# Experts of a mixture ranked by token count on the chip, six light ones in plain float32 on two column tiles

## The chip, the cores and the metric

The kernel runs on one core of one Trainium2 chip. The metric is the device time of one execution in microseconds, as the median of several runs. TensorE (PE) multiplies, VectorE (DVE), ScalarE (ACT) and GpSimd (POOL) work on elements, SyncE (SP) issues most of the transfers, and 16 DMA engines move the data.

## What is computed

A trunk of two residual layers over 512 tokens of 1024 channels. Layer 0 mixes tokens by a state-space scan and a pooling mixer, layer 1 by stick-breaking attention. After each mixer comes a mixture of 16 experts, and that is where the change lies:

```
for i in range(DEPTH):                                  # DEPTH = 2
    ...
    x = layer_norm(DEEPNORM_ALPHA * x + mix, ln_mix_g[i], ln_mix_b[i])
    ple = (p[i] @ ple_w_proj[i]) * sigmoid(x @ ple_w_gate[i])
    ffn = grouped_moe(x, router_w, router_bias, moe_w1[i], moe_w3[i], moe_w2[i])
    x = layer_norm(DEEPNORM_ALPHA * x + ffn + ple, ln_ffn_g[i], ln_ffn_b[i])

def grouped_moe(...):                                   # gates: best group of 4, its best 2 experts
    h = silu(einsum('td,edf->etf', xt, w1)) * einsum('td,edf->etf', xt, w3)
    h = h * gates.T[:, :, None]
    y = einsum('etf,efd->td', h, w2)
```

An expert has w1 and w3 of 1024 x 512 and w2 of 512 x 1024, all float32. Each token goes to two experts, so 1024 pairs of token and expert are spread over 16 experts in each layer.

## The kernel before

The reference is in float32. The kernel makes each product of three matmuls in the faster format fp32r: every operand is split into a rounded high part and a low part that holds the rest (`split`, line 81: ScalarE copies the high part, VectorE subtracts), and `mm3` (line 85) adds high x high, high x low and low x high in PSUM.

`route` (line 797 on) works out for every token its two experts, counts the tokens of each expert by a matmul with ones, and `lists` (line 897) turns this into a list of rows for each expert. An expert has CAP = 96 places; entries past its last token point out of bounds, and transfers skip them. If any expert has more than 96 tokens, a flag is set and `overflow` (line 1131, a branch of all engines after expert 12) works off the rest; otherwise the branch only costs its test.

`ffn` (line 915) writes x to a buffer `xd` in DRAM, GpSimd gathers an expert's rows from there into `xgs` (`gather`), `load_g` transposes them on PE and splits them into `g`. For each expert, `up` multiplies with w1 and w3 (two halves of the 1024 channels, kh, into two PSUM banks), `act` makes silu(h1) x h3, `turn` transposes the result, `down` multiplies with w2 (two halves of the output), and `scatter` writes the rows to `yd`. The loop at line 1043 overlaps two experts: while expert e goes through act, turn and down, the first half of up of expert e+1 is multiplied, and the second half after that. The experts come in the order 0 to 15. After expert 7 stands a block of the ple gate (`gate`, GATES); after the loop the rows of `yd` are loaded and added.

Weights come in units of 1 MB (128 x 2048 float32), six for an expert: w1 and w3 for each kh, and two halves of w2. `plan_ffn` (line 1223) lists the units in the order of use, `prefetch` (line 95) issues their loads on SP in that order, LA = 6 units ahead of use (3 from expert 13 on), and `weights` (line 109) splits a unit in two halves into ring buffers. Units lie in the pool `raw` of 17 slots, which X (4 slots), xt (2), xg, pT and g (2) share. A load waits in SP's queue until its slot has been read out, which for a unit of weights is the end of its split. Every address is known when the program is built, so loads may run ahead of the routing.

`plain` (line 474) is like `weights`, without a split: the unit is read from its slot as float32.

## Time and profile before

| | us |
|---|---|
| median of three runs | 1232.31 (1230.9 to 1234.02) |
| the profiled execution | 1232.32 |
| its span | 1230.7 |
| PE busy | 1162.8 (94%) |
| VectorE busy | 959.1 (78%) |
| ScalarE busy | 750.9 (61%) |
| GpSimd busy | 134.9 (11%) |

The profile gives busy time by engine, and, in 40 slices of the span, the busy share of each engine and of the DMA engines in tenths, with the bytes that these moved. A busy PE here includes the drain of each matmul, which overlaps the next one, so matmuls are timed from the start of one to the start of the next. "Waits" put the idle time before an instruction down to the one that released it. PEclk is the clock granted to TensorE, 1.00 for 2.4 GHz and 0.50 for 1.2 GHz.

### The profile page before, as it was taken

The numbers are of one execution on the slowest core, as the hardware profiler recorded it, in microseconds if no ns is written. First come the engines' busy times: TensorE is split into PE (matmuls) and PEld (weight loads), VectorE is DVE, ScalarE is ACT, GpSimd is POOL, SyncE is SP. The second block draws the span as 40 slices with busy tenths as digits, with TensorE's granted clock in tenths as the row PEclk, the third lists the DMA queues.
The fourth block names the chain that finished last, engine by engine and source line by source line (L and its number), as shares of the span: only waits on it lengthen the run. The fifth ranks groups of instructions, "written<-read, shape, count | busy, mean of one in ns | idle before, by whom it ended". The sixth has DMA issues, their size and how long they took to land. (4 is left out here: it accounts for less than half of the span.)

```text
span 1230.7 us, 17431 instructions
## 1 busy us (share of the span) xinstructions
PE 1162.8 (94%) x6479; PEld 888.6 (72%) x6479; DVE 959.1 (78%) x1381; ACT 750.9 (61%) x1063; POOL 134.9 (11%) x150
## 2 busy tenths in 40 slices
PE   6967999999999999999999999999999999999995
PEld 4856779777768776777777767688877767777674
DVE  6997866798986998785576467755799896989786
ACT  4322542688876888763465456523488885888761
POOL 5010020111010101100000000011101100011101
PEclk9998999999999999999999999998999999999998
DMA  8225662599996998972121024434299998899971
GB/s 254 69 78 184 223 232 97 183 372 377 379 377 247 357 388 325 355 283 69 35 76 63 1 69 153 150 145 163 61 361 387 385 378 304 287 397 356 305 276 70
DMA packets 158166, 285.13 MB, mean 232 GB/s; under 512 B 19584, under 2 KB 43664, under 8 KB 157008
## 3 DMA queue, kind: packets, MB, share of 16 engines
q1 hardware_dynamic: 143760, 256.56, 58.5%
q0 software_dynamic: 9568, 25.19, 6.0%
q10 hardware_dynamic: 4736, 2.10, 0.6%
q8 instruction: 55, 0.90, 0.3%
q14 instruction: 47, 0.39, 0.1%
HBM read 272.02 MB, written 20.19 MB: 237 GB/s over the span
## 5 line engine op out<-in xcount | busy, mean ns | idle before, releaser
L83 DVE TENSOR_TENSOR w_0l<-raw,w_0h 128x1024 fp32r<-128x1024 f32 (+1 forms) x233 | 280.0, 1202 | 53.7 <-ACT w_0h L82 49.4
L82 ACT ACTIVATE w_0h<-raw 128x1024 fp32r<-128x1024 f32 (+1 forms) x233 | 242.5, 1041 | 41.2 <-PE pA L89 22.2
L83 DVE TENSOR_TENSOR w_2l<-raw,w_2h 128x1024 fp32r<-128x1024 f32 x205 | 249.8, 1218 | 15.9 <-ACT w_2h L82 15.5
L82 ACT ACTIVATE w_2h<-raw 128x1024 fp32r<-128x1024 f32 x205 | 216.6, 1057 | 49.7 <-PE pA L89 40.3
L87 PE MATMUL pA<-w_0h,g 128*96 128x512 f32 x256 | 104.2, 407 | 0.8 <-ACT g L82 0.7
L88 PE MATMUL pA<-w_0l,g 128*96 128x512 f32 x256 | 101.2, 395 | 1.8 <-DVE w_0l L83 1.8
L89 PE MATMUL pA<-w_0h,g 128*96 128x512 f32 x256 | 101.5, 397 | 0.3 <-DVE g L83 0.3
L89 PE MATMUL pA<-w_2h,g 128*96 128x512 f32 x256 | 101.5, 397 | 0.0
L87 PE MATMUL pA<-w_2h,g 128*96 128x512 f32 x256 | 101.1, 395 | 0.0
L88 PE MATMUL pA<-w_2l,g 128*96 128x512 f32 x256 | 100.3, 392 | 0.0
L979 POOL DMA_INDIRECT yd<-ysb,ixm x30 | 37.7, 1256 | 441.9 <-ACT ysb L1052 421.4
L89 PEld LDWEIGHTS pA<-w_0h,g 128*96 128x96 f32 x256 | 41.3, 161 | 18.8 <-DVE g L83 2.1
L88 PEld LDWEIGHTS pA<-w_2l,g 128*96 128x96 f32 x256 | 41.5, 162 | 17.9
L89 PEld LDWEIGHTS pA<-w_2h,g 128*96 128x96 f32 x256 | 41.3, 161 | 18.0
L87 PEld LDWEIGHTS pA<-w_2h,g 128*96 128x96 f32 x256 | 41.3, 161 | 17.7
L88 PEld LDWEIGHTS pA<-w_0l,g 128*96 128x96 f32 x256 | 41.6, 163 | 17.2 <-DVE w_0l L83 3.8
L973 POOL DMA_INDIRECT xg<-xd,ixm x32 | 37.4, 1170 | 149.0 <-PE pT L995 79.1
L87 PEld LDWEIGHTS pA<-w_0h,g 128*96 128x96 f32 x256 | 41.5, 162 | 15.7 <-ACT g L82 3.1
L87 PE MATMUL pB<-w_0h,sT 128*96 128x512 f32 x128 | 50.7, 396 | 1.2 <-ACT sT L82 1.2
L679 DVE TENSOR_TENSOR_SCAN kw<-kw 128x128 f32<-128x128 f32 (+3 forms) x64 | 50.2, 813 | 0.9 <-ACT kw L676 0.6
L88 PE MATMUL pB<-w_0l,sT 128*96 128x512 f32 x128 | 50.5, 394 | 0.4 <-DVE w_0l L83 0.4
L89 PE MATMUL pB<-w_0h,sT 128*96 128x512 f32 x128 | 50.8, 397 | 0.0
(442 smaller groups left out, 2810.9 us busy)
## 6 DMA issues: line engine op xcount, KB each, us to landing
raw<-in_moe_w_dram SPq DMA_DIRECT2D x192, 1024.0 KB, 10.1
raw<-in_sb_w_qkv_dram SPq DMA_DIRECT2D x12, 1024.0 KB, 5.1
raw<-in_ple_w_gate_dram SPq DMA_DIRECT2D x8, 1024.0 KB, 8.4
yt<-yd SPq DMA_DIRECT2D x8, 1024.0 KB, 8.1
raw<-in_ab_w_out_dram SPq DMA_DIRECT2D x4, 1024.0 KB, 6.4
xd<-x0r POOLq DMA_DIRECT2D x8, 512.0 KB, 4.1
raw<-in_sb_w_out_dram SPq DMA_DIRECT2D x4, 1024.0 KB, 5.6
raw<-in_ab_w_in_dram SPq DMA_DIRECT2D x3, 1024.0 KB, 7.7
```

The lines of the kernel that those rows point to most:

```text
L82: return (self.nc.scalar.activation(hi, src, AF.Copy), (self.nc.gpsimd if pool else self.nc.vector).tensor_tensor(lo, src, hi.bitcast(F32) ...
L83: (self.nc.gpsimd if pool else self.nc.vector).tensor_tensor(lo, src, hi.bitcast(F32), op=OP.subtract))
L87: t.matmul(out, s[0], m[0], start=first, stop=False)
L88: t.matmul(out, s[0], m[1], start=False, stop=False)
L89: t.matmul(out, s[1], m[0], start=False, stop=last)
L679: v.tensor_tensor_scan(rv, rv, rv, 1.0, op0=OP.mult, op1=OP.min)
L973: return nc.gpsimd.indirect_dma_start(out=xgs[:CAP, e % 2, :], out_offset=None, in_=xd[:, :], in_offset=bass.IndirectOffsetOnAxis(ap=self. ...
L979: nc.gpsimd.indirect_dma_start(out=yd[:, :], out_offset=bass.IndirectOffsetOnAxis(ap=self.iy[:CAP, e:e + 1], axis=0), in_=src[:CAP], in_of ...
```

## The change

After the counts are known, `route` ranks the experts by them on VectorE: `key` is 16 x count plus a tie-break, raised for experts 0 and 1 so that they take ranks 1 and 2 always; `rank` is the number of keys that are at least as large. The lists are made by rank instead of by expert (`val`), and `order` holds, as integers, the expert of each rank. The loop goes through ranks in the order of SEQ, so that position 0 and 1 are experts 0 and 1, and ranks 11 to 16, the light ones, stand at positions 2, 5, 8, 10, 12 and 14. A light expert has 64 places instead of 96; the flag of the overflow counts 32 more for it.

Since which expert has rank 3 to 16 is known only on the chip, `expert` reads its index from `order` into a register of SP, and `prefetch` issues the loads of its weights at an address made from it. Loads of experts 0 and 1 stay as they were.

A light expert is not split: its gathered rows are copied out of PSUM as float32 (one half by ScalarE, the other by VectorE), the weights are read by `plain`, and `up` multiplies each 128 channels of g with w1 and with w3 in turn, one to PSUM partitions 0 to 63, the other to 64 to 127 of the same bank: two tiles of 64 columns of the array. `down` does the same with the two halves of w2. A slot of weights is now free when PE has read it. `last_onehot` and `overflow` use the ranks too. Cut to what matters:

```diff
+SMALL = 64
+BIG = 10
+SEQ = (1, 2, 11, 3, 4, 12, 5, 6, 13, 7, 14, 8, 15, 9, 16, 10)
...
+            if callable(ap):
+                ap = ap()
+                if ap is None:
+                    break
...
+        self.kb = cp.tile([128, 16], F32, name="kb")
+        nc.vector.tensor_copy(self.kb, self.w16)
+        for e in range(2):
+            nc.vector.tensor_scalar(self.kb[:, e:e + 1], self.kb[:, e:e + 1], float((2 - e) << 15), None, op0=OP.add)
...
-        v.tensor_reduce(red[:, 0], pp[:, 64:80], AX.X, OP.max)
-        self.flag = cp.tile([128, 1], I32, tag="flag", bufs=2, name=f"flag{layer}")
-        v.tensor_scalar(self.flag, red[:, 0], CAP + 0.5, None, op0=OP.is_gt)
-        keep = cp.tile([128, 2, NT, 17], F32, tag="keep", bufs=1, name=f"keep{layer}")
-        pos = keep[:, :, :, 16:17]
...
+        key, rank, cap = f(16), f(16), f(16)
+        cmp = rt[:, 0:256].rearrange("p (a b) -> p a b", a=16)
+        val = rt[:, 256:384].rearrange("p (k i e) -> p k i e", k=2, i=NT)
+        sq16 = [128, 16, 16]
+        v.scalar_tensor_tensor(key, pp[:, 64:80], 16.0, self.kb, op0=OP.mult, op1=OP.add)
+        v.tensor_tensor(cmp, key[:, None, :].to_broadcast(sq16), key[:, :, None].to_broadcast(sq16), op=OP.is_ge)
+        v.tensor_reduce(rank, cmp, AX.X, OP.add)
+        fk = lambda ap: ap.rearrange("p k i e -> p (k i) e")
+        bc8 = [128, 2 * NT, 16]
+        v.tensor_tensor(fk(val), fk(m), rank[:, None, :].to_broadcast(bc8), op=OP.mult)
+        v.tensor_reduce(fk(rk), fk(val), AX.X, OP.add)
+        v.tensor_tensor(fk(val), self.slotrow[:, None, :16].to_broadcast(bc8), fk(rk).to_broadcast(bc8), op=OP.is_equal)
+        for k in range(2):
+            v.tensor_tensor(val[:, k], val[:, k], self.tokv[:, :, k:k + 1].to_broadcast(bc16), op=OP.mult)
...
-        self.val = val = keep[:, :, :, :16]
-        for k in range(2):
-            v.tensor_tensor(val[:, k], m[:, k], self.tokv[:, :, k:k + 1].to_broadcast(bc16), op=OP.mult)
...
-        self.lists(0, tiles)
+        self.lists(pos, val, tiles)
+        v.tensor_tensor(cmp, self.slotrow[:, :16][:, :, None].to_broadcast(sq16), rank[:, None, :].to_broadcast(sq16),
+                        op=OP.is_equal)
+        v.tensor_tensor(cmp, cmp, self.w16[:, None, :].to_broadcast(sq16), op=OP.mult)
+        v.tensor_reduce(key, cmp, AX.X, OP.add)
+        order = cp.tile([128, 16], I32, tag="order", bufs=1, name=f"order{layer}")
+        v.tensor_scalar(order, key, -1.0, 16.0, op0=OP.mult, op1=OP.add)
+        self.order[layer] = order
+        v.tensor_scalar(cap, rank, BIG + 0.5, float(CAP - SMALL), op0=OP.is_gt, op1=OP.mult)
+        v.tensor_tensor(cap, cap, pp[:, 64:80], op=OP.add)
+        v.tensor_reduce(red[:, 0], cap, AX.X, OP.max)
+        self.flag = cp.tile([128, 1], I32, tag="flag", bufs=2, name=f"flag{layer}")
+        v.tensor_scalar(self.flag, red[:, 0], CAP + 0.5, None, op0=OP.is_gt)
...
+    def expert(self, layer, r):
+        if layer not in self.order:
+            return None
+        if (layer, r) not in self.eid:
+            self.eid[layer, r] = self.nc.values_load(
+                self.order[layer][0:1, r - 1:r], engines=[mybir.EngineType.SP], min_val=0, max_val=NE - 1,
+                skip_runtime_bounds_check_because="the ranks are a permutation, so the value is an index of an expert")
+        return self.eid[layer, r]
...
+        def rows(e):
+            return SMALL if SEQ[e] > BIG else CAP
...
-                out=xgs[:CAP, e % 2, :], out_offset=None, in_=xd[:, :],
-                in_offset=bass.IndirectOffsetOnAxis(ap=self.ix[:CAP, e:e + 1], axis=0),
+                out=xgs[:c, e % 2, :], out_offset=None, in_=xd[:, :],
+                in_offset=bass.IndirectOffsetOnAxis(ap=self.ix[:c, r:r + 1], axis=0),
...
-            g = self.slot(f"g{layer}_{e}", F32R)[:, :2 * KB * CAP].rearrange("p (a k t) -> p a k t", a=2, k=KB)
+            c = rows(e)
+            if c == CAP:
+                g = self.slot(f"g{layer}_{e}", F32R)[:, :2 * KB * c].rearrange("p (a k t) -> p a k t", a=2, k=KB)
+            else:
+                g = self.slot(f"g{layer}_{e}")[:, :KB * c].rearrange("p (k t) -> p k t", k=KB)
...
+                if c == CAP:
+                    self.split(g[:, 0, ks], g[:, 1, ks], p)
+                elif hf:
+                    v.tensor_copy(g[:, ks], p)
+                else:
+                    nc.scalar.activation(g[:, ks], p, AF.Copy)
...
+        def banks(e):
+            return [self.bank("A", "pA") for _ in range(2 if rows(e) == CAP else 1)]
+
+        def up(eg, hh, kh, a):
+            e, g = eg
+            if rows(e) == CAP:
+                w = self.weights(LA)
+                for k in range(4):
+                    kb = kh * 4 + k
+                    self.mm3(hh[a][:CAP], (g[:, 0, kb], g[:, 1, kb]), w[k], kb == 0, kb == KB - 1)
+                return
+            if a == 0:
+                self.pair = [self.plain(LA), self.plain(LA)]
+            for k in (2 * a, 2 * a + 1):
+                kb = kh * 4 + k
+                for x in range(2):
+                    nc.tensor.matmul(hh[0][x * 64:x * 64 + 64], g[:, kb], self.pair[x][:, k], start=(kb == 0),
+                                     stop=(kb == KB - 1))
...
+            nc.scalar.activation(t[64:128, :512], hh[0][0:64], AF.Silu)
+            sg = t[0:64, 512:]
+            v.tensor_tensor(sg, t[64:128, :512], hh[0][64:128], op=OP.mult)
+            return sg
...
+                sT = self.half4("sT")[:, :4 * c].rearrange("p (k t) -> p k t", k=4)
+                v.tensor_copy(sT, p)
...
+            w = [self.plain(LA), self.plain(LA)]
+            py = self.bank("B", "pB")
             for k in range(4):
-                nc.tensor.transpose(p[:, k * CAP:(k + 1) * CAP], t[:CAP, k * 128:(k + 1) * 128], self.ident[:CAP, :CAP])
-            self.split(sT[:, 0], sT[:, 1], p.rearrange("p (k t) -> p k t", k=4))
-            return sT
-
-        def down(sT):
-            for nh in range(2):
-                w = self.weights(LA)
-                py = self.bank("B", "pB")[:CAP]
-                for k in range(4):
-                    self.mm3(py, (sT[:, 0, k], sT[:, 1, k]), w[k], k == 0, k == 3)
-                yield slice(nh * 512, (nh + 1) * 512), py
+                for x in range(2):
+                    nc.tensor.matmul(py[x * 64:x * 64 + 64], sT[:, k], w[x][:, k], start=(k == 0), stop=(k == 3))
+            for x, h in enumerate(hs):
+                yield h, py[x * 64:x * 64 + 64]
...
+        def part(e, n, rs, cs=slice(None)):
+            r = SEQ[e]
+            if r <= 2:
+                return I[n][layer, r - 1, rs, cs]
+
+            def dyn():
+                x = self.expert(layer, r)
+                return None if x is None else I[n][layer, bass.ds(x, 1), rs, cs]
+            return dyn
...
-                self.plan(I[n][layer, e, kh * 512:(kh + 1) * 512, :], 4, 512)
+                self.plan(part(e, n, slice(kh * 512, (kh + 1) * 512)), 4, 512)
...
-                self.plan(I["moe_w2"][layer, e, :, nh * 512:(nh + 1) * 512], 4, 512)
+                self.plan(part(e, "moe_w2", slice(None), slice(nh * 512, (nh + 1) * 512)), 4, 512)
```

On PE, the stretch around expert position 2 of layer 0 (g_2: its rows; pA: the bank of up; raw: a weight slot; w: a split half) was before, from the turn of expert 1 on:

```order
L1020 MATMUL pT<-ident,sg 128x96 x4
L87 MATMUL pA<-w_0h,g_2_2264 96x512
L88 MATMUL pA<-w_0l,g_2_2264 96x512
L89 MATMUL pA<-w_0h,g_2_2264 96x512
...
L87 MATMUL pA<-w_2h,g_2_2264 96x512
L88 MATMUL pA<-w_2l,g_2_2264 96x512
L89 MATMUL pA<-w_2h,g_2_2264 96x512
```

and is now, from the end of the heavy expert 1's up (g_1) to its down (pB):

```order
L94 MATMUL pA<-w_2h,g_1_2112 96x512
L1072 MATMUL pA<-raw_2180,g_2_2284 64x512
L1072 MATMUL pA<-raw_2210,g_2_2284 64x512
L1091 MATMUL pT<-ident,sg 128x96 x4
L1072 MATMUL pA<-raw_2210,g_2_2284 64x512
L1072 MATMUL pA<-raw_2180,g_2_2284 64x512
L1072 MATMUL pA<-raw_2210,g_2_2284 64x512
L92 MATMUL pB<-w_0h,sT 96x512
```

Eight plain matmuls, w1 and w3 in turn, stand where 24 split ones stood, and the transposes of the expert before (sg) lie among them.

On SP, the loads of the same place (raw: weight units in the order of use) were before:

```order
L105 DMA raw_5291<-in_ple_w_proj_dram 128x2x256
L105 DMA raw_2133<-in_moe_w_dram 128x4x512
L105 DMA raw_2160<-in_moe_w_dram 128x4x512
L105 DMA raw_2190<-in_moe_w_dram 128x4x512
L105 DMA raw_2213<-in_moe_w_dram 128x4x512
```

and are now:

```order
L114 DMA raw_4750<-in_ple_w_proj_dram 128x2x256
L114 DMA raw_2150<-in_moe_w_dram 128x4x512
L934 TENSOR_LOAD order_1815
L114 ISA
L114 DMA raw_2180<-in_moe_w_dram 128x4x512
L114 ISA
L114 DMA raw_2210<-in_moe_w_dram 128x4x512
L114 DMA raw_2233<-in_moe_w_dram 128x4x512
```

The register read stands ahead of the first load of each rank from 3 on, and each load by register has one more instruction (ISA) before it; the order of the units is the same.

On VectorE, the stretch from the counts (pT) to the lists (oh) in route was before:

```order
L868 TENSOR_REDUCE rt<-pT 128x1
L875 TENSOR_TENSOR rt<-rt,pT 128x64
L870 TENSOR_SCALAR flag_1772<-rt 128x1
L876 TENSOR_REDUCE keep_1774<-rt 128x4
L875 TENSOR_TENSOR rt<-rt,pT 128x64
L909 TENSOR_SCALAR oh<-slotrow,keep_1774 128x128
L876 TENSOR_REDUCE keep_1774<-rt 128x4
L909 TENSOR_SCALAR oh<-slotrow,keep_1774 128x128 x7
```

and is now:

```order
L889 SCALAR_TENSOR_TENSOR rt<-pT,kb 128x16
L900 TENSOR_TENSOR rt<-keep_1747,pT 128x64
L890 TENSOR_TENSOR rt<-rt 128x256
L901 TENSOR_REDUCE keep_1747<-rt 128x4
L891 TENSOR_REDUCE rt<-rt 128x16
L900 TENSOR_TENSOR rt<-keep_1747,pT 128x64
L894 TENSOR_TENSOR rt<-keep_1747,rt 128x128
L895 TENSOR_REDUCE keep_1747<-rt 128x8
L947 TENSOR_SCALAR oh<-slotrow,keep_1747 128x128
L896 TENSOR_TENSOR rt<-slotrow,keep_1747 128x128
L898 TENSOR_TENSOR rt<-rt,tokv 128x64 x2
L947 TENSOR_SCALAR oh<-slotrow,keep_1747 128x128 x6
```

The ranks (L889 to L898) moved in ahead of most of the lists' comparisons, and the reduction for the flag moved behind them.

## Rows read from the trace of the kernel before

**Rows 1.** Page, part 2: busy tenths of PE and of the DMA engines, 40 slices.

```profile
PE   6967999999999999999999999999999999999995
DMA  8225662599996998972121024434299998899971
```

**Rows 2.** By stretch: length, busy PE, PEld, DVE, ACT, POOL, clock, DMA share, GB/s.

```profile
232.00:240.00 8.00, 8.00 (x41) 5.75 (x40) 6.46 (x8) 7.41 (x10) 1.48 (x1) 1.00 0.89 269
232.00:522.00 290.00, 287.90 (x1427) 208.38 (x1425) 250.01 (x259) 234.95 (x283) 35.77 (x30) 1.00 0.98 352
240.00:380.00 140.00, 138.78 (x669) 98.88 (x668) 124.80 (x124) 115.46 (x139) 17.33 (x15) 1.00 1.03 377
380.00:393.00 13.00, 13.00 (x105) 12.44 (x105) 4.91 (x8) 5.37 (x8) 0.98 (x1) 1.00 0.35 130
393.00:400.00 7.00, 7.00 (x35) 4.95 (x34) 6.57 (x10) 6.79 (x8) 0.00 (x0) 1.00 0.84 259
400.00:480.00 80.00, 80.00 (x378) 56.90 (x377) 73.73 (x73) 67.67 (x82) 9.26 (x9) 1.00 1.03 372
480.00:490.00 10.00, 9.12 (x47) 6.18 (x46) 8.24 (x10) 8.37 (x11) 0.91 (x1) 1.00 0.65 227
530.00:540.00 10.00, 10.00 (x72) 9.04 (x71) 8.94 (x9) 4.85 (x7) 0.00 (x0) 1.00 1.01 414
889.00:1179.00 290.00, 286.21 (x1419) 207.24 (x1418) 248.22 (x258) 233.71 (x282) 34.62 (x29) 1.00 0.97 350
```

**Rows 3.** Timeline of ScalarE at two successive silus: start us, us, engine, line, operation.

```profile
271.28 0.59 ACT L1012 ACTIVATE sg<-pA 96x512 f32<-96x512 f32 x1 [0.20 <-PE pA L89]
...
288.95 0.59 ACT L1012 ACTIVATE sg<-pA 96x512 f32<-96x512 f32 x1 [0.20 <-PE pA L89]
```

**Rows 4.** Page, part 6: loads of the experts' weights, KB each, us to landing.

```profile
raw<-in_moe_w_dram SPq DMA_DIRECT2D x192, 1024.0 KB, 10.1
```

**Rows 5.** Waits of SP's queue, 232 to 522 us: total us, times, longest us.

```profile
SPq L105 <- DVE w_2l L83: 204.4, 65, 24.7
...
SPq L1135 <- SPq L1135: 12.7, 1, 12.7
```

**Rows 6.** Loads of line 105 issued from 232 to 522 us.

```profile
DMA to landing us min/median/max: 5.4/11.5/14.2
```

**Rows 7.** Loads of line 105 issued from 555 to 770 us.

```profile
DMA to landing us min/median/max: 5.0/5.1/8.4
```

**Rows 8.** Timeline of PE: first and last of 24 matmuls of a down.

```profile
351.00 0.39 PE L87 MATMUL pB<-w_0h,sT 128*96 128x512 f32 x1
...
356.34 0.39 PE L89 MATMUL pB<-w_2h,sT 128*96 128x512 f32 x1
```

**Rows 9.** Timeline of PE: plain float32 over the whole array, four in a row.

```profile
549.31 1.88 PE L1097 MATMUL pA<-yt,dg 128*128 128x512 f32 x4
```

**Rows 10.** Timeline of PE: plain float32 on two column tiles, and the next matmul.

```profile
796.26 1.09 PE L691 MATMUL pA<-kw,v 128*64 128x128 f32 x14
797.27 0.50 PE L87 MATMUL pA<-w_2h,oh 128*128 128x512 f32 x1
```

**Rows 11.** Timeline of PE: first matmul of the gate block, and first behind it.

```profile
376.00 0.28 PE L87 MATMUL pG<-w_0h,cath 128*128 128x256 f32 x1
...
391.01 0.45 PE L87 MATMUL pA<-w_0h,g 128*96 128x512 f32 x1
```

**Rows 12.** Timeline of PE and VectorE in the routing: first gather's transposes, list comparisons.

```profile
222.53 0.85 PE L995 MATMUL pT<-ident,xg 96*128 96x96 f32 x8 [1.03 <-DMA xg<-xd,ixm]
212.95 1.45 DVE L909 TENSOR_SCALAR oh<-slotrow,keep 128x128 f32<-128x128 bf16 x7
```

**Rows 13.** SP's reads of the overflow flag into a register: duration ns.

```profile
L1133 SPq TENSOR_LOAD <-flag x2: 297/396/494, 470.6 to 1128.4; - x2
```

**Rows 14.** By stretch, PE only: length, busy PE, clock, DMA share, GB/s.

```profile
70.00:75.00 5.00, 2.48 (x11) 1.00 0.00 0
95.00:100.00 5.00, 0.08 (x1) 0.50 0.94 300
```

More of the change, by code (lines that the diff above doesn't have):

```diff
@@ L52, in __init__ @@
         self.cat = None
+        self.order = {}
+        self.eid = {}
     def dbg(self, name, ap):
@@ L847, in route @@
         v.tensor_tensor(ge(sm), ge(sel), fl(t2)[:, :, None].to_broadcast(b44), op=OP.min)
-        m = f(2, NT, 16)
+        keep = cp.tile([128, 2, NT, 18], F32, tag="keep", bufs=1, name=f"keep{layer}")
+        self.m = m = keep[:, :, :, :16]
+        self.pos = pos = keep[:, :, :, 16:17]
+        self.rk = rk = keep[:, :, :, 17:18]
         e16 = f(NT, 16)
@@ L909, in lists @@
                 v.tensor_scalar(oh[:, x], self.slotrow, pos[:, k, i], None, op0=OP.is_equal)
-                nc.tensor.matmul(pl[:, :16], oh[:, x], self.val[:, k, i], start=(x == 0), stop=(x == 2 * NT - 1))
+                nc.tensor.matmul(pl[:, :16], oh[:, x], val[:, k, i], start=(x == 0), stop=(x == 2 * NT - 1))
         v.tensor_scalar(pf, pl[:, :16], 0.5, self.padv, op0=OP.is_lt, op1=OP.mult)
@@ new lines, in down @@
+        def down(e, sT):
+            hs = [slice(nh * 512, (nh + 1) * 512) for nh in range(2)]
+            if rows(e) == CAP:
+                for h in hs:
+                    w = self.weights(LA)
+                    py = self.bank("B", "pB")[:CAP]
+                    for k in range(4):
+                        self.mm3(py, (sT[:, 0, k], sT[:, 1, k]), w[k], k == 0, k == 3)
+                    yield h, py
+                return
+            w = [self.plain(LA), self.plain(LA)]
+            py = self.bank("B", "pB")
+            for k in range(4):
+                for x in range(2):
+                    nc.tensor.matmul(py[x * 64:x * 64 + 64], sT[:, k], w[x][:, k], start=(k == 0), stop=(k == 3))
+            for x, h in enumerate(hs):
+                yield h, py[x * 64:x * 64 + 64]
@@ L1036, in ffn @@
             pass
-        hh = [self.bank("A", "pA"), self.bank("A", "pA")]
+        hh = banks(0)
         up(g, hh, 0, 0)
@@ L1044, in ffn @@
             LA = 6 if e < 13 else 3
-            sg = act(hh)
-            hh = [self.bank("A", "pA"), self.bank("A", "pA")]
+            sg = act(e, hh)
+            hh = banks(e + 1)
             up(gn, hh, 0, 0)
-            sT = turn(sg)
+            sT = turn(e, sg)
             up(gn, hh, 0, 1)
             ysb = self.half4("ysb")
-            for h, py in down(sT):
-                nc.scalar.activation(ysb[:CAP, h], py, AF.Copy)
+            for h, py in down(e, sT):
+                nc.scalar.activation(ysb[:rows(e), h], py, AF.Copy)
             scatter(e, ysb)
@@ L1146, in overflow @@
             nc.gpsimd.memset(xo, 0.0)
+            pos = tiles[2][:, 8:].rearrange("p (k i o) -> p k i o", k=2, o=1)
+            for k in range(2):
+                v.tensor_tensor(self.m[:, k], self.m[:, k], self.tokv[:, :, k:k + 1].to_broadcast([128, NT, 16]),
+                                op=OP.mult)
             for kk in range(NT):
-                self.lists(CAP + kk * 128, tiles, wb[:, :1024], pt)
+                v.tensor_scalar(pos, self.rk, BIG + 0.5, float(CAP - SMALL), op0=OP.is_gt, op1=OP.mult)
+                v.scalar_tensor_tensor(pos, pos, -float(CAP + kk * 128), self.pos, op0=OP.add, op1=OP.add)
+                self.lists(pos, self.m, tiles, wb[:, :1024], pt)
                 ld = self.dp.tile([128, 32], I32, name=f"ld{layer}_{kk}")
```

59 lines of the change are left out of this document (30 added, 29 removed).

## Prediction

> **What bounds the kernel now.** I read the page first, then the table by stretches, then the rows behind it. The page's slices show PE at 9 tenths nearly everywhere, and DMA at 9 in the same slices, 9 to 17 and 30 to 38, and low elsewhere [rows 1]: in the two expert loops (about 232 to 522 us and 889 to 1179 us) two resources are full at once. The table by stretches says the same more sharply [rows 2]. From 240 to 380 us PE is busy 138.8 of 140 us, and the DMA engines have a share of 1.03 at 377 GB/s. VectorE and ScalarE are busy 250 and 235 of the loop's 290 us, so they don't bind. An expert takes 17.67 us, from one silu to the next [rows 3]. Its weights are six loads of 1.05 MB [rows 4]; with 1024 rows of 4 KB gathered and scattered by 16 experts it moves 6.29 + 0.52 = 6.81 MB, which at 377 GB/s is 18.1 us. So the transfers need about as long as PE does, and a PE that is made faster will find itself waiting for weights.
>
> Two more views bear this out. The loads' queue waits for a slot to be freed by a split (204 us in the loop) [rows 5], so PE's pace sets when a load may start; but a load then takes 11.5 us to land in the loop [rows 6] against 5.1 us in the attention stage [rows 7], where one is under way at a time. Three to four are always in flight, and the transfer queue is not empty.
>
> **The light expert on PE.** Before, an expert is 72 passes in fp32r (24 weight blocks, three each). 24 of them start between 351.00 and 356.34 us, 23 steps of 0.232 us [rows 8]: 72 x 0.232 = 16.7 us, and the transposes make the 17.67. After, a light expert has 24 plain float32 matmuls, which the chip runs as two passes each (two matmuls of L1097 stand as four) [rows 9]: 48 passes. A plain pass of 512 columns over the whole array takes (1.88 - 0.59)/3 = 0.43 us, 0.59 being one alone. Two column tiles side by side are in the attention stage already: 14 passes of 128 columns on tiles of 64, alternating, take 1.09 us, so (1.09 - 0.27)/13 = 0.063 us each [rows 10], where a quarter of 0.43 would be 0.107. The two tiles do run together. For 512 columns I take 0.43/2 = 0.216 us, since the row's steps hold pauses between groups; four times 0.063 = 0.25 is the upper end. A light expert is then 48 x 0.216 = 10.4 us (12.1), against 16.7: 6.3 us (4.6) off, 12 times in two layers, **76 us (55) of PE work removed**. The 144 VectorE and 144 ScalarE split halves that go were hidden behind PE and give nothing.
>
> The edges between tile shapes cost something. After the last of the 14 tiled passes (796.26 + 13 x 0.063 = 797.08 us) the next matmul starts at 797.27, 0.19 us later where a pass takes 0.06 [rows 10]: about 0.1 us a change of shape, some eight in a light expert, 0 to 14 us in all. The Trainium skill, TensorEngine Tiling (Array Packing), Key Properties, speaks against this change here: changing the tiling mode drains the engine. The 0.19 us agree; by that rule the PE work removed would be 62 us rather than 76. In the sum it weighs nothing as long as PE has time to spare.
>
> **What the loads leave of it.** The change removes no load and no byte: padded list entries are out of bounds before and after. So the end of each loop moves only by what the DMA engines stand below full rate. Layer 0 moves 290 x 0.352 = 102.1 MB [rows 2]; at 377 GB/s that is 270.8 us, 19.2 below 290. Layer 1 moves 290 x 0.350 = 101.5 MB: 269.2, 20.8 below. **40 us of slack in all.** Where it lies in layer 0: 8 us at the start at 269 GB/s (2.3 lost), the gate block (13 us at 130 and 7 at 259 GB/s: 8.5 + 2.2), the branch of the overflow (10 us at 227: 4.0).
> - Start: experts 0 and 1 stay heavy and go at PE's pace: 2.5 a layer stay.
> - Gate block: PE spends 15.0 us on it [rows 11], all slots fill and loads stop. After, PE is short of weights when it gets there, so the slots are empty: 17 slots less 4 for X, 2 for xt, one each for xg and pT and two for g leave seven, 7 x 2.75 = 19 us of loads at 382 GB/s against 15 and a split; the first load after it starts from an empty queue (5.1 us [rows 7]). I leave 3 of 10.7.
> - Branch: SP stands there 12.7 us [rows 5] and issues nothing. Short of weights, PE reaches it sooner after SP does, with loads still in flight: 1 of 4.0 stays.
> That leaves 6.5 a layer, 13 in all, and 27 us are gained at 377 GB/s.
>
> **The rate itself** is the largest unknown. 377 and 372 GB/s are the rates in the loop, with PE 99 to 100% busy beside them and freeing the slots, so the engines were not asked for more. The most in any stretch is 414 GB/s, for loads alone (530 to 540 us, the rows of yd) [rows 2]. The loop's rows are the nearest, the same mix; I take 382, an estimate five above them. Then the slack is 22.7 + 24.3 = 47, less 13: 34 us.
>
> **Added on the routing path.** The ranks put some ten small VectorE instructions between the counts and the lists, of up to 256 columns; a row of 128 takes 0.2 us in a stream (7 in 1.45), so 1.5 to 2.5 us, of which some lies beside other work. PE already waits 1.03 us for the first gather there [rows 12]. I take 1.5 a layer, 3 us; 0 to 5 as bounds. The values that follow the lists (order, flag) have until the first load by register, which waits for a slot far later. SP gains 14 register reads a layer, 0.3 to 0.5 us each [rows 13], and one short instruction with each load; behind them stand the next loads, and SP waits over 200 us for slots, so nothing while three or more are in flight; without that cover 28 x 0.4 = 11 us.
>
> **Sum.** 34 - 3 = 31 us off the profiled execution's 1232.32, which is the median of the runs to 0.01: **1201 us**. With 372 GB/s, 19 us staying, and 5 for routing: (15.5 + 17.2) - 19 - 5 = 9, so 1223. With 395: (31.5 + 33.0) - 13 = 51, so 1181.
>
> **Rivals.**
> - *The loads give way and PE binds again.* If the engines move 414 GB/s in the mix too, the slack is 43 + 45 = 88 us, more than PE's 76. Then the gain is 76 - (0 to 14) - 3: 1159 to 1173 us. For it: PE was as busy as DMA. Against: landing at 11.5 us, over twice the 5.1. The Trainium skill, DMA: Bandwidth & Descriptors, Specifications, gives a fabric ceiling of 435 GB/s and a limit of about 358 per core from HBM; by the first an expert's 6.81 MB would take 15.7 us (an estimate) and this rival would hold, by the second nothing would be gained. The rows lie between, 377 held for 140 us, so neither is the figure here.
> - *Slower: loads by register.* 14 experts of each layer, 168 loads, take their address from a register, and no row of before shows such a load. On the path that binds, 31/168 = 0.18 us more for each uses up the gain. If each cost 0.4 us more, as long as a register read [rows 13], it is 67 us: 1268. For: nothing hides there once loads bind. Against: the page's queue table lists SP's loads as hardware_dynamic already, and the extra work is on SP, which waits.
> - *Slower: the clock falls in light experts.* PE would work some 11.5 of 18 us there. In 95 to 100 us, PE as good as idle, the clock is 0.50, its lower level of 1.2 GHz; in 70 to 75, 2.48 of 5 us busy, it is 1.00 [rows 14]. At the lower level a light expert takes 48 x 0.43 = 20.6 us and 1 for transposes, 3.5 over the loads' pace, 12 times 42: 1243. The busier row says no.
> - *The tiles don't run together at 512 columns*: the change does not do what it says. 20.6 against 16.7 us, 12 x 4 = 47: 1279. The tiled passes of the attention stage speak against it [rows 10].
>
> An overflow does not occur: with the reference's inputs the eleventh expert in rank has 61 tokens or fewer in both layers.
>
> **How the numbers follow.** Loads bind, 1181 to 1223: 0.70. PE binds, 1159 to 1173: 0.15. Loads by register: 0.08. Clock: 0.04. Tiles: 0.03. Some 0.05 of the first case lies past its bounds, within 0.3% of before (1228.6 to 1236.0, about what a measurement of this kernel can tell from no change): faster 0.80, same 0.05, slower 0.15. The range runs from 1166, in the middle of the second case, to 1223: it leaves out the slower rivals, 0.15, and the 0.05.
>
> **What would show it.** Passes of a light expert in pairs that start together, 0.216 us a pass; DMA at 1.0 or more and 375 to 390 GB/s through both loops with no dip at the gate block; PE idle before the plain matmuls, released by loads of moe_w, some 6 us for each light expert; heavy experts as before. PE near full and over 395 GB/s would mean the first rival; loads landing more than 0.2 us further apart than 2.8, the second. The prediction fails if the engines' rate in the mix, which I read from stretches where PE was full too, is not their limit.

## The result: slower by 22 us

| kernel | median us | runs | ratio to before |
|---|---|---|---|
| before | 1232.69 | 4 | |
| after | 1254.82 | 4 | 1.0179, 95% interval 1.0160 to 1.0198 |

The prediction was 1201 us, with a range of 1166 to 1223 and 0.80 for faster. Its direction is wrong: the interval lies wholly above 1. The profiled execution of after took 1255.37 us; its span is 1253.7 at a mean granted clock of 0.960 (before 0.985).

The page of after, parts 1, 2, 5 and 6; in part 5 the numbers behind the bar are busy us, mean ns of one, and the idle time before it with its releaser:

```profile
PE 1138.2 (91%) x6191; PEld 795.7 (63%) x6191; DVE 790.1 (63%) x1252; ACT 594.4 (47%) x895; POOL 127.8 (10%) x150
...
PE   5986998999899887999999999998999899997885
...
DMA  8225563599998996973112024434299999998861
...
L92 PE MATMUL pA<-w_0h,g 128*96 128x512 f32 x160 | 71.1, 444 | 32.5 <-ACT g L87 28.0
...
raw<-in_moe_w_dram SPq DMA_DIRECT2D x192, 1024.0 KB, 11.6
```

DMA is at 9 in nearly the same slices as before [rows 1], PE now falls to 8 and 7 there, and a load of an expert takes 11.6 us to land where it took 10.1 [rows 4]. PE waits 32.5 us in front of the first products of heavy blocks, and 28.0 of these end with ScalarE's split of the gathered rows (g). Nearly all of these waits lie in the heavy units behind a light one (a heavy or light unit is here an expert's turn in the loop). One of the longest in layer 0, on PE, then ScalarE's queue ahead of it, then PE's stretch behind it:

```profile
330.70 0.62 PE L92 MATMUL pA<-w_0h,g 128*96 128x512 f32 x1 [5.01 <-ACT g L87]
```

```profile
326.38 1.06 ACT L87 ACTIVATE w_0h<-raw 128x1024 fp32r<-128x1024 f32 x1
...
330.18 0.85 ACT L87 ACTIVATE g<-pT 128x384 fp32r<-128x384 f32 x2
```

```profile
331.00:337.00 6.00, 5.44 (x13) 2.92 (x11) 2.12 (x3) 1.67 (x3) 0.00 (x0) 0.50 1.05 387
```

From 325.77 us on ScalarE makes the silu of the light unit, four weight splits and the split of g, one behind the other, and waits for no load between them; PE stands until the last. So this wait is for ScalarE's queue and not for a load. PE's clock then falls to 0.50, the lower level, and 13 passes stand 0.43 us apart instead of 0.23: some 2.5 us more (an estimate from these steps). Waits of 5.0, 3.1 and 5.0 us stand in both layers, at positions 6, 11 and 13. No wait of the plain matmuls ends with a load.

The table by stretches of after, beside [rows 2] (length, busy PE, PEld, DVE, ACT, POOL, clock, DMA share, GB/s):

```profile
232.00:240.00 8.00, 8.00 (x42) 5.79 (x41) 7.70 (x10) 6.45 (x9) 1.51 (x2) 1.00 0.40 119
232.00:522.00 290.00, 268.28 (x1269) 160.05 (x1268) 163.06 (x183) 155.87 (x197) 31.96 (x30) 0.96 0.95 337
240.00:380.00 140.00, 133.20 (x603) 79.40 (x602) 89.77 (x93) 85.18 (x106) 17.09 (x15) 0.98 1.04 370
380.00:390.00 10.00, 10.00 (x80) 9.07 (x79) 4.01 (x7) 5.65 (x8) 2.07 (x2) 1.00 0.96 356
390.00:400.00 10.00, 10.00 (x69) 7.34 (x68) 6.34 (x9) 3.88 (x5) 0.00 (x0) 1.00 0.46 148
400.00:480.00 80.00, 71.28 (x315) 38.64 (x316) 38.09 (x42) 37.43 (x48) 8.24 (x8) 0.94 1.04 374
480.00:490.00 10.00, 9.89 (x43) 4.97 (x41) 2.95 (x4) 3.85 (x5) 0.92 (x1) 1.00 0.50 171
490.00:500.00 10.00, 3.90 (x16) 1.59 (x16) 3.37 (x4) 2.43 (x4) 0.00 (x0) 0.74 0.51 169
510.00:520.00 10.00, 10.00 (x59) 5.97 (x58) 4.08 (x6) 6.50 (x10) 2.13 (x3) 1.00 0.68 222
```

The loop as a whole moves less per microsecond than before (337 against 352 GB/s). In its middle the loads run at the old rate (370 and 374 against 377 and 372) with the DMA share at 1.04. What is new lies at 480 to 500 and 510 to 520 us, around the branch of the overflow and in the tail: some 170 and 222 GB/s. The same stretches of before, and its gate block, which [rows 2] cuts otherwise:

```profile
380.00:390.00 10.00, 10.00 (x87) 10.00 (x87) 2.53 (x5) 2.41 (x4) 0.00 (x0) 1.00 0.46 169
390.00:400.00 10.00, 10.00 (x53) 7.39 (x52) 8.95 (x12) 9.75 (x12) 0.98 (x1) 1.00 0.59 181
...
490.00:500.00 10.00, 10.00 (x56) 7.57 (x55) 9.74 (x16) 8.54 (x11) 1.18 (x1) 1.00 1.03 388
510.00:520.00 10.00, 10.00 (x46) 6.79 (x45) 7.93 (x8) 7.58 (x10) 0.00 (x0) 1.00 1.04 390
```

ScalarE's silus in the timeline of after, at positions 2 (light), 3, 4, 5 (light) and 6, then 13, 14 (light) and 15:

```profile
276.93 0.59 ACT L1082 ACTIVATE sg<-pA 64x512 f32<-64x512 f32 x1 [1.99 <-PE pA L1072]
290.37 0.60 ACT L1079 ACTIVATE sg<-pA 96x512 f32<-96x512 f32 x1 [0.33 <-PE pA L94]
308.76 0.59 ACT L1079 ACTIVATE sg<-pA 96x512 f32<-96x512 f32 x1 [3.00 <-PE pA L94]
325.77 0.59 ACT L1082 ACTIVATE sg<-pA 64x512 f32<-64x512 f32 x1 [3.69 <-PE pA L1072]
348.35 0.59 ACT L1079 ACTIVATE sg<-pA 96x512 f32<-96x512 f32 x1
...
487.15 0.59 ACT L1079 ACTIVATE sg<-pA 96x512 f32<-96x512 f32 x1 [0.80 <-PE pA L94]
518.28 0.59 ACT L1082 ACTIVATE sg<-pA 64x512 f32<-64x512 f32 x1
536.83 0.59 ACT L1079 ACTIVATE sg<-pA 96x512 f32<-96x512 f32 x1 [2.68 <-PE pA L94]
```

The first light unit does save time: 13.4 us to the next silu instead of 17.7 [rows 3], with 17.9 ahead of it, so a heavy and a light unit take 31.3 us and not 35.3. The second one gives it back: 22.6 us from 325.77 to 348.35. The wait for ScalarE shown above and the slow passes behind it make up most of the 9 us between the two. Another reading, tested below: the first light unit used up loads that lay ready, and from then on the loads set the pace. Then the branch: 31.1 us from position 13 to 14 and 18.6 to 15, where before took 24.4 and 16.0:

```profile
481.75 0.59 ACT L1012 ACTIVATE sg<-pA 96x512 f32<-96x512 f32 x1 [0.29 <-PE pA L89]
...
506.12 0.59 ACT L1012 ACTIVATE sg<-pA 96x512 f32<-96x512 f32 x1
522.09 0.60 ACT L1012 ACTIVATE sg<-pA 96x512 f32<-96x512 f32 x1 [0.42 <-PE pA L89]
```

### The profile page after: what moved, and what is told of

The parts are those of the page before. It is cut to its first block, busy times and chain, and to the rows that moved or that the text cites. A ratio compares the mean times of both kernels' runs of the same rounds, so it can differ in the third digit from the quotient of the medians.

```text
span 1253.7 us, 16680 instructions
## 1 busy us (share of the span) xinstructions
PE 1138.2 (91%) x6191; PEld 795.7 (63%) x6191; DVE 790.1 (63%) x1252; ACT 594.4 (47%) x895; POOL 127.8 (10%) x150
## 5 line engine op out<-in xcount | busy, mean ns | idle before, releaser
L88 DVE TENSOR_TENSOR w_0l<-raw,w_0h 128x1024 fp32r<-128x1024 f32 (+1 forms) x161 | 192.2, 1194 | 72.9 <-ACT w_0h L87 72.1
L87 ACT ACTIVATE w_0h<-raw 128x1024 fp32r<-128x1024 f32 (+1 forms) x161 | 166.4, 1033 | 74.2 <-DMA raw<-in_moe_w_dram 34.7
L88 DVE TENSOR_TENSOR w_2l<-raw,w_2h 128x1024 fp32r<-128x1024 f32 x133 | 162.0, 1218 | 39.8 <-ACT w_2h L87 39.8
L87 ACT ACTIVATE w_2h<-raw 128x1024 fp32r<-128x1024 f32 x133 | 139.7, 1051 | 30.9 <-PE pA L94 28.7
L92 PE MATMUL pA<-w_0h,g 128*96 128x512 f32 x160 | 71.1, 444 | 32.5 <-ACT g L87 28.0
L1072 PE MATMUL pA<-raw,g 128*64 128x512 f32 x384 | 99.6, 621 | 0.0
L1139 ACT ACTIVATE ysb<-pB 96x512 f32<-96x512 f32 (+1 forms) x60 | 35.7, 594 | 97.7 <-PE pB L1115 56.3
L94 PE MATMUL pA<-w_0h,g 128*96 128x512 f32 x160 | 68.0, 425 | 2.1 <-DVE g L88 2.0
L92 PE MATMUL pA<-w_2h,g 128*96 128x512 f32 x160 | 65.9, 412 | 0.0
L94 PE MATMUL pA<-w_2h,g 128*96 128x512 f32 x160 | 65.2, 408 | 0.0
L92 PEld LDWEIGHTS pA<-w_0h,g 128*96 128x96 f32 x160 | 27.9, 174 | 56.6 <-ACT g L87 35.1
L1115 PE MATMUL pB<-raw,sT 128*64 128x512 f32 x192 | 46.0, 599 | 0.0
L88 DVE TENSOR_TENSOR w_4l<-raw,w_4h 128x1024 fp32r<-128x1024 f32 x20 | 24.4, 1221 | 24.6 <-ACT w_4h L87 24.3
## 6 DMA issues: line engine op xcount, KB each, us to landing
raw<-in_moe_w_dram SPq DMA_DIRECT2D x192, 1024.0 KB, 11.6
```

Of the source, the lines that this page charges most:

```text
L87: return (self.nc.scalar.activation(hi, src, AF.Copy), (self.nc.gpsimd if pool else self.nc.vector).tensor_tensor(lo, src, hi.bitcast(F32) ...
L88: (self.nc.gpsimd if pool else self.nc.vector).tensor_tensor(lo, src, hi.bitcast(F32), op=OP.subtract))
L92: t.matmul(out, s[0], m[0], start=first, stop=False)
L94: t.matmul(out, s[1], m[0], start=False, stop=last)
L1072: nc.tensor.matmul(hh[0][x * 64:x * 64 + 64], g[:, kb], self.pair[x][:, k], start=(kb == 0), stop=(kb == KB - 1))
L1115: nc.tensor.matmul(py[x * 64:x * 64 + 64], sT[:, k], w[x][:, k], start=(k == 0), stop=(k == 3))
```

## The experiments

All times are medians. Ratios and differences to before are against its own median in the same set of runs (1232.6 to 1233.5 us); two other kernels are compared by their medians.

**Loads by register** (a_static): every load at a constant address, the rank order of these inputs as a table.

```diff
...
-            if r <= 2:
-                return I[n][layer, r - 1, rs, cs]
+            if r:
+                return I[n][layer, ORD[layer][r - 1], rs, cs]
```

> The kernel after with one thing undone: every expert's loads take a constant address (the rank order of these inputs written into the program), so no register is read and no load is made by register; ranks, lists, light and heavy units and their order stay. Theory 1 (the loads still bind, and the 22 us are DMA time that stands idle around the branch and in the loop's tail, plus some 5 us at the first layer's start): within 4 us of after, 1251 to 1258. Theory 2 (loads by register are slower, 168 x 0.13 to 0.18 us): 1225 to 1235.

1253.49 us, ratio 1.0165 (1.0136 to 1.0193). After is 1.0179: the registers cost 1.3 us by the medians, which can't be told from nothing, and by the two intervals not more than some 6. Theory 2, which needs 20, falls.

**Ranks and registers without light units** (a_heavy): `BIG = 16`.

> The kernel after with the other thing undone: the ranks, the alternating order and the loads by register stay, but all sixteen experts are worked as heavy ones (BIG = 16, so no unit counts as light): fp32r products as in before. Theory 1: before plus what the ranks cost, 1234 to 1242. Theory 2: near after, 1250 or more. If ranks alone cost the 5 us seen at the first layer's first silu, twice: 1242 to 1245.

1236.90 us, 1.0042 (1.0026 to 1.0058): 4.3 over before. So light units with all that follows from them cost 18 us, though they take work from PE.

**The branch** (a_nobranch, b_nobranch): in both kernels the two lines that call the overflow are left out.

> The kernel after without the branch of the overflow in both layers (left out: the work on experts with more tokens than their rows, which these inputs don't need; the flag is still computed). Theory 1: the 17 to 24 us without a load around the branch come back for the most part, 8 to 14 us a layer: 1227 to 1239, and the difference to before without the branch is 12 us or less. Rival (the loss is in the tail, with 3 instead of 6 loads ahead, or spread over the loop): falls by no more than before without it does, 1240 to 1250.

> The kernel before without the branch of the overflow in both layers (left out as in the run of after without it). Its cost in before: the 10 us at 227 GB/s and PE's 0.8 us there; expected 2 to 8 us less than before, 1225 to 1231. If after without it falls by 10 us more than this, the branch is where light units lose; if both fall alike, it isn't.

After without it: 1238.26, 1.0048 (1.0027 to 1.0069). Before without it: 1226.69, 0.9955 (0.9939 to 0.9970). The branch costs 16.5 us in after and 5.9 in before; half of the 22 us is its. In the loops nothing is left: from first to last silu 284.5 us in both layers, before without it 283.8 and 283.9. Without the branch light units neither gain nor lose there.

**A constant made on another engine** (a_kb). The first silu of layer 0 comes 5.3 us late in after, but PE is already 4.7 us late in its first transposes. VectorE's timeline at the program's start, then GpSimd's, then PE's, in after:

```profile
5.36 0.23 DVE L451 RECIPROCAL band<-band 128x16 f32<-128x16 f32 x1
12.67 0.17 DVE L167 COPY kb<-w 128x16 f32<-128x16 f32 x1 [7.08 <-POOL w L164]
```

```profile
12.47 0.16 POOL L164 IOTA w<- 128x16 f32 x1
```

```profile
13.51 0.90 PE L181 MATMUL pT<-ident,x 128*128 128x128 f32 x3 [4.64 <-ACT s5sm L248]
```

kb, which the ranks need at 217 us, is written in the code ahead of the first mixer. Its copy waits 7.08 us for an iota that stands far back in GpSimd's queue, and what VectorE owes the mixer stands behind it. The edit:

```diff
-        nc.vector.tensor_copy(self.kb, self.w16)
+        nc.gpsimd.tensor_copy(self.kb, self.w16)
-            nc.vector.tensor_scalar(self.kb[:, e:e + 1], ...
+            nc.gpsimd.tensor_scalar(self.kb[:, e:e + 1], ...
```

> The kernel after with the constant kb of the ranks made on GpSimd, behind the iota it copies, instead of on VectorE. In the trace of after VectorE stands 7.08 us at that copy, behind it the start of the first mixer, and the first silu of layer 0 comes 5.3 us later than before. Theory: that wait is 4 to 5 us of the whole time (the ranks themselves about 1): 1249 to 1251. Rival (the ranks on the routing path cost the 5 us, the wait at the start is made up later): 1253 or more.

1244.14 us, 1.0082 (1.0065 to 1.0099): 10.7 less than after, more than twice what was expected. At the first silu of layer 0 only 2.9 us of it show (239.31 instead of 242.22).

**The same in the kernel without light units** (a_hkb):

> The kernel of the run a_heavy (ranks, alternating order, loads by register, all experts in fp32r products) with kb made on GpSimd. Theory: what was left of a_heavy's 4.3 us over before was that wait: 1232 to 1235, so ranks and loads by register cost 0 to 2 us. Rival (the ranks cost it on the routing path): 1236 or more.

1230.78 us, 0.9991 (0.9977 to 1.0005), 1.2 under the range. With kb out of the way, ranks and loads by register together can't be told from nothing. kb is worth 6.1 us here, against 10.7 in after (and 6.6 and 4.4 in two pairs below, a_seq2 and a_seqkb, a_over7 and a_mix). Part of the rest shows at the branch. VectorE's branch and the first entry behind it in after (first and last are layers 0 and 1), then in a_kb:

```profile
L1222 DVEq COMPARE_BRANCH  x2: 63/68/72, 490.7 to 1157.2; - x2
...
L1222 DVEq EVENT_SEMAPHORE  x2: 21/21/21, 496.4 to 1163.1; - x2
```

```profile
L1222 DVEq COMPARE_BRANCH  x2: 63/68/72, 486.1 to 1151.0; - x2
...
L1222 DVEq EVENT_SEMAPHORE  x2: 21/21/21, 491.4 to 1151.6; - x2
```

VectorE needs 5.7 and 5.9 us to get on behind the branch in after, 5.3 and 0.6 in a_kb. In layer 1 the interval of silus across the branch falls from 30.7 to 26.3 us with it: 4.3 of the 4.6 us between the two prices of kb. How a constant of the program's start should shorten that crossing is not shown.

**The branch at another place** (a_over7, b_over7): `OVER = 7`, ahead of the block of the per-layer gate.

> The kernel after with the branch of the overflow behind expert position 7, ahead of the block of the per-layer gate, instead of behind position 12 (OVER = 7). Theory: SP's stop at the branch then falls beside work of PE that needs no loads, and a heavy and a light unit of the tail no longer stand around it; the branch's cost of 16.5 us falls to 2 to 8: 1240 to 1248. Rival (the cost lies in the engines' start after the branch wherever light units alternate): 1252 or more.

> The kernel before with the branch behind position 7, ahead of the gate block. Its cost at position 12 is 5.9 us. Theory: the two stretches of idle DMA (branch and gate block) become one; 0 to 5 us less than before, 1227 to 1233. Rival: 1236 or more, because PE's start after the branch is no longer covered.

After: 1231.95, 0.9990 (0.9979 to 1.0000), 23 us less, 8 under the range, and less even than without a branch. Before: 1245.74, 1.0100 (1.0083 to 1.0117), 12 us more, a miss; the rival, 1236 or more, held. With the branch there the two gaps in the loads of after become one. Two stretches of a_over7:

```profile
380.00:390.00 10.00, 9.85 (x68) 7.57 (x67) 4.58 (x5) 6.37 (x8) 1.09 (x1) 1.00 0.67 232
390.00:400.00 10.00, 10.00 (x80) 8.83 (x78) 4.56 (x7) 4.47 (x6) 0.99 (x1) 1.00 0.87 321
```

Loads refill while PE works on the gate block; the interval behind position 10 is 13.8 us, 18.3 in after. In b_over7 PE leaves the branch after standing 5.2 us, its clock is then 0.54 (385 to 390 us), and the loads have a second gap (0 GB/s from 400 to 405 us): two gaps as before, and a PE that has no time to spare for either. Why a_over7 is also 6 us below a_nobranch was not settled.

**PE a third** (b_third): the kernel before with one of each three products.

```diff
-                self.mm3(hh[a][:CAP], (g[:, 0, kb], g[:, 1, kb]), w[k], kb == 0, kb == KB - 1)
+                nc.tensor.matmul(hh[a][:CAP], g[:, 0, kb], w[k][0], start=(kb == 0), stop=(kb == KB - 1))
```

and the same for the down product.

> The kernel before with a third of the experts' products: of each triple of fp32r products only the first is made (the two correction products of up, gate and down are left out); loads, splits, slots, ring, branch and order stay. PE then needs about 6 us for an expert's products instead of 16.7, so the time is what the loads and their slots allow. Theory (the engines are at their limit at 370 to 377 GB/s in the mix, and stretches without loads stay): 1200 to 1222. Rival (the rate was set by PE's pace and the engines give 400 GB/s or more): 1150 to 1185.

1222.39 us, 0.9914 (0.9897 to 0.9930), 0.4 above the range of its theory. Stretches of b_third:

```profile
232.00:522.00 290.00, 188.17 (x689) 110.85 (x689) 248.34 (x260) 228.00 (x284) 40.50 (x29) 0.72 0.97 353
240.00:380.00 140.00, 89.47 (x297) 50.84 (x296) 121.29 (x123) 109.24 (x137) 20.98 (x16) 0.70 1.03 384
380.00:390.00 10.00, 10.00 (x83) 9.81 (x82) 4.03 (x7) 3.55 (x6) 0.00 (x0) 1.00 0.30 112
390.00:400.00 10.00, 8.00 (x41) 5.42 (x40) 9.38 (x12) 9.66 (x12) 0.00 (x0) 0.83 0.81 263
```

PE is busy 188 of 290 us, at a clock of 0.72, and the loop moves 353 GB/s, as before (352). The gap at the gate block is still there (112 and 263 GB/s, before 169 and 181). With far more taken from PE than the change takes, the whole gets 11 us shorter, and 6.7 of them lie ahead of the two first silus. From the first silu to the last the loops take 283.5 and 283.2 us, before 285.2 and 287.1: 1.7 and 3.9 us are all that a faster PE finds there. VectorE, busy 248 of 290 us with the splits, could hold this kernel too; but the loops of a_mix below, with 165 us of VectorE, take 284.8 and 282.6.

**Fewer bytes in light units** (a_half, built on a_mix below):

```diff
-                self.pair = [self.plain(LA), self.plain(LA)]
+                self.pair = [self.plain(LA)] * 2
-            for n in ("moe_w1", "moe_w3"):
+            for n in ("moe_w1", "moe_w3")[:1 if SEQ[e] > BIG else 2]:
```

> The kernel of the run a_mix with two of a light expert's six loads left out (w3 isn't loaded: both column tiles take w1, so the products are as many as before, but the second one is of the wrong matrix). 24 loads of 1.05 MB, 25.2 MB less; PE's work, the slots and the branch as in a_mix. Theory (the loads bind in light units): at 373 GB/s up to 67 us less than a_mix, of which PE's own pace leaves 45 to 67: 1160 to 1183. Rival (light units are held by PE, its waits between passes or the slots, not by bytes): 1205 or more.

A light unit's w3 isn't loaded; both tiles take w1. 1185.60 us, 0.9629 (0.9613 to 0.9644), 42 less than a_mix and 2.6 above the range. Three silus of a_half, heavy, light, heavy (positions 4 to 6), and a stretch of its loop:

```profile
302.91 0.60 ACT L1079 ACTIVATE sg<-pA 96x512 f32<-96x512 f32 x1 [0.34 <-issue]
320.74 0.59 ACT L1082 ACTIVATE sg<-pA 64x512 f32<-64x512 f32 x1 [2.91 <-PE pA L1072]
334.21 0.59 ACT L1079 ACTIVATE sg<-pA 96x512 f32<-96x512 f32 x1 [0.33 <-PE pA L94]
```

```profile
400.00:480.00 80.00, 80.00 (x366) 42.88 (x363) 45.59 (x56) 43.04 (x56) 9.39 (x9) 1.00 0.96 339
```

The same light unit that took 22.6 us to the next silu in after takes 13.5 here, and PE is busy 80 of 80 us. PE's work is the same, but more than the bytes differs: fewer slots are taken, and in the order of ScalarE's queue, which is fixed with the program, the split of g now stands ahead of the light unit's silu, so that PE's waits of 5 us are gone. So a_half doesn't tell the loads from ScalarE's order, and no run moves that order alone. A heavy and a light unit now take 31.3 us where two heavy ones took 35.3: 4.0 us is what a light unit is worth when PE is free to run, 48 for twelve.

How much can hang on ScalarE's order? The loads were at a share of 1.04 while PE stood. 15 units of 6.81 MB take 273 us at the 374 GB/s of after and 263 at the 388 that b_third has from 250 to 340 us. If the engines give no more than that, it is at most some 10 us a layer (an estimate from these rates), less than half of the 24 that six light units take from PE; the rest is then put down to the loads.

**Both edits that helped** (a_mix: kb on GpSimd and `OVER = 7`), **six loads ahead in the tail** (a_mix6: `LA = 6`), and **other positions of the light units** (a_seq2, a_seqkb, a_seq7):

```diff
-SEQ = (1, 2, 11, 3, 4, 12, 5, 6, 13, 7, 14, 8, 15, 9, 16, 10)
+SEQ = (1, 2, 11, 3, 12, 4, 13, 5, 14, 6, 15, 16, 7, 8, 9, 10)
```

> The kernel after with both edits that helped alone: kb made on GpSimd and the branch ahead of the gate block (OVER = 7). Theory: the wait at the start (3 us at the first silu of layer 0) and the idle loads around the branch are apart in time, so they add: 1232 less 3 to 6, 1225 to 1229, faster than before. Rival (both were one effect on the loads' phase in the loop, or the gain is eaten by the loads' limit): 1231 or more.

> The kernel of the run a_mix with six loads ahead in the tail too (LA = 6 instead of 3 from position 13 on). Theory (the tail's intervals in the runs without a branch are those of before, so the look-ahead isn't what binds): within 3 us of a_mix. Rival (three light loads ahead are too few): 4 to 10 us less than a_mix.

> The kernel after with the light units at positions 2, 4, 6, 8, 10 and 11 instead of 2, 5, 8, 10, 12 and 14, so that the units around the branch (behind position 12) and in the tail are heavy, as in before. Theory (light units use up the loads that lie ready in 10 us instead of 17, so around the branch PE runs dry while the loads stand): the branch costs 6 to 10 instead of 16.5 us, 1244 to 1249. Rival (loads bind wherever light units stand, and what isn't loaded around the branch is missing later in any order): 1252 or more.

> The kernel of the run a_seq2 (light units at 2, 4, 6, 8, 10 and 11, branch behind position 12) with kb made on GpSimd. Theory: kb is worth the 3 us of the first silu and no more where the branch has heavy units around it: 1234 to 1237. Rival: 10 us as in after, 1229.

> The kernel of the run a_mix (kb on GpSimd, branch ahead of the gate block) with the light units at positions 2, 4, 6, 8, 10 and 11, none in the tail. Theory (the order only paid at the branch, and that is gone): within 3 us of a_mix, 1225 to 1231. Rival (heavy units in the tail are worth something by themselves): 1218 to 1224.

| kernel | kb on | branch behind | tail | us | ratio to before |
|---|---|---|---|---|---|
| a_mix | GpSimd | 7 | light units | 1227.59 | 0.9956 (0.9943 to 0.9969) |
| a_mix6 | GpSimd | 7 | light units, 6 loads ahead | 1230.28 | 0.9978 (0.9968 to 0.9987) |
| a_seq2 | VectorE | 12 | heavy | 1239.02 | 1.0046 (1.0034 to 1.0057) |
| a_seqkb | GpSimd | 12 | heavy | 1232.47 | 1.0005 (0.9996 to 1.0015) |
| a_seq7 | GpSimd | 7 | heavy | 1226.24 | 0.9956 (0.9942 to 0.9971) |

a_mix and a_seq7 beat before by 0.4%. The gains don't add: 10.7 and 22.9 us alone, 27.2 together. The look-ahead of 3 isn't what binds in the tail. Moving the branch from 12 to 7 is worth 6.2 us with heavy units around it (a_seqkb less a_seq7) and 16.5 with light ones (a_kb less a_mix). Leaving it out was worth nearly the same, 5.9 in before, where the units around it are heavy, and 16.5 in after. a_seq2 came out 5 us under the range, a_seqkb 1.5 under.

## Why the prediction was wrong

Of the 53.8 us between the forecast and the result, 31.5 are a gain that didn't come: with kb on GpSimd and heavy units around the branch, light units leave the time where it was (a_seqkb, 1.0005). The other 22.3 are kb and the branch. The runs make a chain from before to after: ranks and registers -2.2 us (a_hkb against before, not distinct from 0), light units away from branch and tail +1.7 (a_seqkb less a_hkb, not distinct from 0 either), light units around the branch and in the tail +11.7 (a_kb less a_seqkb), kb on VectorE +10.7 (after less a_kb). Each link ends where the next one starts, so that they add up to 21.9 of the 22.1 us is no proof of them; another order of the edits gives other prices (kb alone has four, from 4.4 to 10.7 us).

- **PE's work: mechanism right, size too big.** In after a light expert's passes stand in pairs that start 0.01 us apart:

```profile
273.20 3.65 PE L1072 MATMUL pA<-raw,g 128*64 128x512 f32 x16
...
276.79 0.47 PE L92 MATMUL pA<-w_0h,g 128*96 128x512 f32 x1
```

  16 passes in 3.59 us are 0.224 each against the 0.216 taken. But 4.0 us a unit came off PE's pace, not 6.3: 48 in all, not 76. In a_half, between 305.58 and 310.64 us, some passes stand alone at 0.427 each, since the order puts one tile's passes away from the other's, and 16 passes take 4.6 us instead of 3.6; the edge between shapes is 0.08 us (the first heavy pass behind takes 0.31 instead of 0.23), as bounded.
- **"What the loads leave of it" is the step that failed.** It took the 40 us in which the DMA engines stand below full rate for time that a faster PE would fill, and let 13 stay. Lost time, the length of a stretch times (1 - share/1.05), in layer 0: at the gate block (380 to 400 us) 10.0 us before (shares 0.46 and 0.59) and 6.5 in after, where 3 were to stay; around the branch and in the tail (480 to 500 and 510 to 520 us) 4.1 before and 13.9 in after, where 1 was to stay; the start (232 to 240) 1.2 and 5.0, since layer 0 comes late. b_third shows that the premise was wrong, not only its sizes: with a third of PE's products the gate block still loses 9.4 us, and both loops together get 5.6 us shorter. What makes the gaps (the order, the branch, the slots) was tried for the branch alone.
- **Heavy units were not "as before".** VectorE and ScalarE were taken as hidden behind PE. Behind a light unit PE has less work to hide ScalarE's splits, and it waits 28.0 us for them in both layers, then runs at the lower clock. The sign "PE idle before the plain matmuls, released by loads" did not show in after at all. What of the missing gain is ScalarE's and what the loads' stays open; the estimate behind a_half gives the loads the larger part.
- **The branch had the opposite sign.** The text let SP's stop cost less, "with loads still in flight". What it missed is the other side: while SP stands, PE lives on the loads that lie ready. PE in after, the last passes of light unit 12, and what follows:

```profile
480.51 3.65 PE L1115 MATMUL pB<-raw,sT 128*64 128x512 f32 x16
...
492.43 0.43 PE L1042 MATMUL pT<-ident,xg 64*128 64x64 f32 x4 [2.54 <-PEq L1222]
496.53 0.66 PE L1042 MATMUL pT<-ident,xg 64*128 64x64 f32 x4 [3.67 <-DVEq L1222]
```

  PE is done with what it has at 489.9 us, then stands for its own way out of the branch and for VectorE's, 6.2 us, and has a clock of 0.50 from 497 to 500 us. Before, PE's queue held matmuls to 483.8 us while it crossed, and it stood 0.8 us:

```profile
484.56 0.85 PE L995 MATMUL pT<-ident,xg 96*128 96x96 f32 x8 [0.77 <-PEq L1135]
```

  SP's queue, 460 to 500 us in after:

```profile
SPq L1222 <- SPq L1222: 11.5, 4, 5.4
SPq L114 <- DVEq L1222: 5.7, 1, 5.7
```

  SP's stop is no longer than it was (11.5 us against 12.7 [rows 5]); the 5.7 us behind it are new, a load that waits for VectorE to cross the branch. The time lost there was not made up; that this is because loads set the pace is argued, not shown.
- **The rate.** 382 GB/s was taken for the mix; after has 370 and 374 at a share of 1.04, b_third 384 (240 to 380 us). The estimate of five above the rows had no row behind it, and 7 of the 34 us hung on it; by b_third it was not far off. The Trainium skill, DMA: Bandwidth & Descriptors, Specifications, gives about 358 from HBM per core, by which nothing was to be gained. The rows stand 3 to 7% above that figure, so it is not the limit here; that light units gained nothing (a_seqkb) agrees with what it forecast, not with the figure.
- **kb was not costed at all.** The sum went through the routing path and took 1.5 us a layer there; the trace agrees on layer 0 (from the counts' last matmuls to the first gather's transposes 10.9 us before, 12.5 in after). The three VectorE instructions for kb stand in the same diff, in another function, and got no line. The edit that moves them is worth 10.7 us in after and 6.1 without light units, half of the 22 us; 2.9 of the 10.7 show at layer 0's first silu and 4.3 at the crossing in layer 1, the rest is spread.
- **The rivals.** Loads by register (0.08): refuted by a_static and a_hkb; pricing SP's reads at nothing was right. Tiles not together (0.03): refuted by the pairs. PE binds again (0.15): only in a_half is PE busy throughout. The clock (0.04): it fell, but not in light units as such. It was 0.50 from 331 to 337 us and from 497 to 500 us, each time after PE had stood 5 or 6 us; what this costs the whole was not tried. No rival held the branch or a wait at the program's start, and the slower side had 0.15.

What stays open: the share of ScalarE's order in the missing gain, why VectorE takes 0.6 us in some crossings and 5.9 in others, how kb reaches the crossing in layer 1, and why a_over7 is faster than no branch.

## What to carry to other kernels

Where two resources are full at once, work taken from one is worth only what the other's gaps give back, and a gap counts as slack only if a run, or a row, shows that the engine made faster is what causes it; a kernel with two thirds of that engine's work left out measures this in one run. A wait counts as one for loads only if the instruction that ends it had itself waited for a load: here it was the last of six in ScalarE's queue. Units with less work on PE made a stop of all engines more costly here (16.5 us against 6), so such units stay away from a branch, or the branch goes to where PE has work that needs no loads. And each new instruction is costed at its place in its engine's queue, a constant at the program's start too: what it waits for stalls all that stands behind it.
